# Last group's matrix-memory output turned by DVE and transfers, and turned blocks read a step later

## The chip, the cores and the metric

One core of a Trainium2 chip runs the kernel. The metric is device time in microseconds (us) of one execution; a profiled execution also leaves a trace of every engine: TensorE (PE, with its weight loads PEld), VectorE (DVE), ScalarE (ACT), GpSimd (POOL) and the queue of SyncE (SP), which issues most transfers.

## The reference, cut to what matters

One decoder layer, 256 tokens by 1024 channels, float32. An input projection feeds two branches: a matrix memory (mLSTM, 4 heads of 256) and an attention (MoBA, 8 heads of 128). Each branch has its own output projection; the two are gated, summed, projected, and followed by a layer norm and a gated MLP.

```python
proj = jnp.einsum("bsd,dn->bsn", x, w_in) + b_in
q_m, k_m, v_m, o_m, i_m, f_m, q_b, k_b, v_b, g_a, g_b = _split_cols(proj, SPLIT_SIZES)
...
h_m = mlstm_chunkwise(...)
y_a = (jax.nn.sigmoid(o_m) * head_norm(h_m, mlstm_norm)).astype(x.dtype)
h_b = moba_attention(...)
merged = (jax.nn.sigmoid(g_a) * jnp.einsum("bsw,wd->bsd", y_a, w_branch_a)
          + jax.nn.sigmoid(g_b) * jnp.einsum("bsw,wd->bsd", y_b, w_branch_b))
return jnp.einsum("bsd,de->bse", merged, w_out)
```

`head_norm` normalises each head's 256 channels of a token. With 256 tokens the attention is one causal block, so it is a plain causal softmax with a bias.

## The kernel before

The weights are a stream of 81 chunks of 128 x 2048 float32 (1 MB each), numbered s, one chunk a step, in a written order. Steps 0 to 3 are the output gate. Then come four groups g = 0 to 3 of eight steps each, from step 4 + 8g: `qm, qb, km, kb, vm, vb, ga, gb`. A group covers one memory head and two attention heads. Steps 36 to 43 are the branch projections (`wa, wa, wb, wb` twice: `wa` for the memory branch, `wb` for the attention), 44 to 47 the output projection, then the MLP.

Every float32 matmul is made of three in a rounded format: a value is split into a high part and the rest, and `mm3` issues high x high, rest x high, high x rest. So each weight chunk goes through `split`: ACT casts `raw` to `wh`, DVE subtracts to `wl`. The buffers `raw`, `wh` and `wl` have three places each. At step s the chunk s + 2 is split and the load of chunk s + 5 is issued on SP's queue; that load takes the place of `raw` of chunk s + 2, so it waits for that split.

All instructions are emitted in program order, by hand. At step s, `elem_work(s)` first emits what ACT, DVE and POOL do: the evacuation of step s - 1 (`evac`), side work put there by the groups (`side_elem`), interleaved with the split parts by the functions in `mixed` (a `None` in such a list stands for the next split part). Then come the load, the matmuls of step s (`step_*`), and the groups' own matmuls (`side_pe`). Each engine, and SP's queue, works in that order; semaphores make it wait.

A group's own work, by the names in `group_schedule`:
- `pe_s`, `el_w`, `el_s`: scores of the memory. `pe_n` makes the numerators `psn0`, `psn1` (tokens on partitions) in PSUM. `el_n1` takes mean, variance and denominator from them, `el_n1b` writes the centred and gated rows `yt` and the scale `scl`, `el_n2` scales `yt` on ACT. The rows must then be turned (channels on partitions) into `yah` and `yal` by `el_y`; the first `wa` step multiplies them, two 128-columns of each group.
- `pe_l(i)`, `el_l(i)`, `el_e(i)`, `el_l2(i)`: logits and softmax `lg` of attention head i. The block is turned, `el_t(i)` splits it into `pth`, `ptl`, `ptf`, `pe_o` multiplies them with the values into `pso`, `el_o` writes `ybh`, `ybl` for the `wb` steps.

A block is turned by `turn(i)` (i = 0, 1 the attention heads, 2 the memory): DVE transposes 32 x 32 tiles into `turn`, SP writes that to `flip` in DRAM, and four reads bring it back in its place. The reads are queued on SP right behind the write and wait until it has landed. In group 3 the memory's rows are not turned in this way: `pe_y` transposes them by four PE matmuls into `psy`, between steps 35 and 36.

`pe_o` stands behind the matmuls of the tenth step from the group's start, in group 3 behind those of the ninth, step 36.

Of the kernel before, what the change touches and what calls it, by code (L numbers as in the profile page):

```python
# [18 lines left out]
P = 128  # L19
S = 256  # L20
D = 1024
KT = D // P
# [50 lines left out]
class Kernel:  # L73
# [69 lines left out]
    def mm3(self, ps, ah, al, bh, bl, start, stop, first=None, only=(0, 1, 2)):  # L143

        a = (ah if first is None else first, ah, al)
        b = (bh, bl, bh)
        for i in only:
            self.nc.tensor.matmul(ps, a[i], b[i], start=start and i == 0, stop=stop and i == 2)  # L148

# [30 lines left out]
    def run(self):  # L180
# [132 lines left out]
        for s, (kind, i) in enumerate(self.order):  # L313
            if kind == "qm":
# [7 lines left out]
                      for i, (m, n) in enumerate(((1, 3), (1, 3), (2, 2))[:3 if g < NG - 1 else 2])] for g in range(NG)]  # L322
# [15 lines left out]
        for s, (kind, i) in list(enumerate(self.order))[4:]:  # L338
# [25 lines left out]
            parts = [] if late else self.split_parts(s + 2)  # L364
            if s == first["wa"] - 1:
                self.kept, parts = parts[-1], parts[:-1]
# [269 lines left out]
    def turn(self, t, d):  # L636
# [7 lines left out]
        self.nc.sync.dma_start(d.rearrange("m p f -> p m f"), tmp.rearrange("p (m f) -> p m f", m=m))  # L644
        t = t.rearrange("p c s -> p (c s)").rearrange("p (k f) -> p k f", k=4 * m)
# [4 lines left out]
    def group_schedule(self, g):  # L650
# [93 lines left out]

        def turn(i):
            self.turn(st["p", i] if i < 2 else st["yt"].rearrange("p t (j d) -> p (t j) d", j=2), self.flip[g][i])

        def pe_y():
            psy = self.ps_side([P, 2, S], f"psy{g}")
            for j in range(2):  # L750
                for t in range(2):
                    nc.tensor.transpose(psy[:, j, t * P:(t + 1) * P], st["yt"][:, t, j * P:(j + 1) * P], self.ident)
            st["psy"] = psy

        def el_y():
            for j in range(2):
                c = 2 * g + j
                gain = self.vec[:, V_NORM + c:V_NORM + c + 1]
                h, l = self.yah[:, c, :], self.yal[:, c, :]
                if last:  # L760
                    y = st["psy"][:, j, :]
                else:
                    y = st["yt"].rearrange("p t s -> p (t s)").rearrange("p (m k) -> p m k", k=64)[:, :, 32 * j:32 * j + 32]
                    h, l = (t.rearrange("p (m i) -> p m i", i=32) for t in (h, l))
                a.activation(h, y, AF.Copy, scale=gain)
                v.scalar_tensor_tensor(l, y, gain, h.bitcast(F32), op0=ALU.mult, op1=ALU.subtract)
# [90 lines left out]
        if g == 0:  # L857
            at(self.side_elem, 6, lambda: self.floor_exp())
        at(self.side_elem, 5 + o, lambda: turn(0))
        self.mixed[b + 6 + o] = lambda w: ([lambda: el_l(1), lambda: el_e(1), el_n1] + w  # L860
                                           + [lambda: el_l2(1), el_n1b, lambda: turn(1)])
        if last:
            self.mixed[b + 7] = lambda w: [el_n2, lambda: el_t(0)] + w
            at(self.side_pe, 7, pe_y)
            self.mixed[b + 8] = lambda w: [el_y, self.kept, lambda: el_t(1)] + w
        else:
# [24 lines left out]
    def step_wa(self, s, c, *a):  # L891
        nc = self.nc
        ps = self.ps_main(f"ps_wa{c}")
        self.mm_feat(s, ps, self.yah, self.yal)

        def evac():
            ga = self.sg["ga"][:, 2 * c:2 * c + 2, :]
            nc.scalar.activation(ga, ga, AF.Sigmoid)
            nc.vector.tensor_mul(ga, ps, ga)
# [421 lines left out]
```

## Time and profile before

| | |
|---|---|
| median of 3 runs | 478.13 us (477.64 to 479.82) |
| profiled execution | 478.69 us, its span 476.7 us |
| PE busy | 469.3 us, 98% of the span |
| DVE busy | 368.1 us, 77% |
| ACT busy | 309.7 us, 65% |
| POOL busy | 37.4 us, 8% |
| transfers | 97.35 MB, 204 GB/s in the mean |

The span is from the first to the last instruction; the execution's time has some 2 us around it. Rows of an engine's timeline read: start in us, length in us, engine, line of the kernel, operation, output<-input, shape, number of instructions merged, and in brackets the idle time before it with what ended it. For SP's queue the length is that of issuing; landing comes later. Rows of the chain that ended last: start, length, engine, output, line, count. Rows of stretches (A:B): length, busy time of PE, PEld, DVE, ACT and POOL, granted PE clock, share of the DMA engines, GB/s. L148 is the one line that issues nearly all matmuls, L94 and L95 the cast and the subtraction of every split, L89 the weight loads, L644 and L648 the write and the reads of a turn.

### The profile page before, as it was taken

The numbers are of one execution on the slowest core, as the hardware profiler recorded it, in microseconds if no ns is written. First come the engines' busy times: TensorE is split into PE (matmuls) and PEld (weight loads), VectorE is DVE, ScalarE is ACT, GpSimd is POOL, SyncE is SP. The second block draws the span as 40 slices with busy tenths as digits, with TensorE's granted clock in tenths as the row PEclk, the third lists the DMA queues.
The fourth block names the chain that finished last, engine by engine and source line by source line (L and its number), as shares of the span: only waits on it lengthen the run. The fifth ranks groups of instructions, "written<-read, shape, count | busy, mean of one in ns | idle before, by whom it ended". The sixth has DMA issues, their size and how long they took to land.

```text
span 476.7 us, 9493 instructions
## 1 busy us (share of the span) xinstructions
PE 469.3 (98%) x3788; PEld 454.8 (95%) x3788; DVE 368.1 (77%) x644; ACT 309.7 (65%) x540; POOL 37.4 (8%) x74
## 2 busy tenths in 40 slices
PE   8999999999999999999999999999999999999994
PEld 6999999999999999999999999999999999999984
DVE  4786979597869786986685898879668666778876
ACT  5669878597859786977663623765555545556871
POOL 0316501000200020010100001000000000000000
PEclk9999999999999999999999999999999999999999
DMA  7985665775666567655967472736564545456202
GB/s 232 324 298 180 212 239 162 222 276 195 173 239 247 193 171 253 234 169 177 368 243 260 148 294 88 268 101 252 184 236 170 206 178 192 171 214 219 89 0 89
DMA packets 28958, 97.35 MB, mean 204 GB/s; under 512 B 10581, under 2 KB 15585, under 8 KB 19697
## 3 DMA queue, kind: packets, MB, share of 16 engines
q1 hardware_dynamic: 27682, 92.51, 55.3%
q0 software_dynamic: 1232, 4.24, 2.7%
q8 instruction: 29, 0.48, 0.4%
q14 instruction: 15, 0.12, 0.1%
HBM read 93.31 MB, written 3.42 MB: 203 GB/s over the span
## 4 chain that ended last, share of the span: by engine, by line
PE 98%; DVE 0%; ACT 0%; DVEq 0%; issue 0%; ACTq 0%
PE ps_up L148 25%; PE ffn L148 13%; PE ps_ga L148 5%; PE ps_kb L148 5%; PE ps_vm L148 5%; PE mix L148 5%; PE ps_km L148 5%; PE ps_gb L148 5%; PE ps_wa L148 5%; PE ps_vb L148 5%; PE ps_wb L148 5%; PE ps_qm L148 5%; PE ps_qb L148 5%; PE ps_o0a L427 1%; PE ps_o0b L427 1%; PE psn L148 1%
## 5 line engine op out<-in xcount | busy, mean ns | idle before, releaser
L95 DVE TENSOR_TENSOR wl<-raw,wh 128x1024 fp32r<-128x1024 f32 (+4 forms) x147 | 180.0, 1261 | 26.8 <-ACT wh L94 24.5
L94 ACT CAST wh<-raw 128x1024 fp32r<-128x1024 f32 (+4 forms) x147 | 151.8, 1077 | 9.3 <-DMA raw<-in_wst_dram 4.0
L148 PE MATMUL ps_up<-x1h,wl 128*128 128x256 f32 x320 | 88.5, 276 | 0.0
L148 PE MATMUL ps_up<-x1h,wh 128*128 128x256 f32 x320 | 88.4, 276 | 0.0
L148 PE MATMUL ps_up<-x1l,wh 128*128 128x256 f32 x320 | 88.4, 276 | 0.0
L148 PEld LDWEIGHTS ps_up<-x1l,wh 128*128 128x128 f32 x320 | 60.1, 188 | 0.4
L148 PEld LDWEIGHTS ps_up<-x1h,wh 128*128 128x128 f32 x320 | 60.1, 188 | 0.3
L148 PEld LDWEIGHTS ps_up<-x1h,wl 128*128 128x128 f32 x320 | 60.1, 188 | 0.0
L1092 DVE SCALAR_TENSOR_TENSOR cu<-ps_up,vec,cu 128x255 f32<-128x255 f32 (+1 forms) x80 | 33.1, 476 | 20.1 <-ACT cu L1088 20.1
L148 PE MATMUL ffn<-wh,hl 128*128 128x512 f32 (+2 forms) x94 | 35.5, 378 | 0.0
L148 PE MATMUL ffn<-wl,hh 128*128 128x512 f32 (+2 forms) x94 | 35.5, 377 | 0.0
L148 PE MATMUL ffn<-wh,hh 128*128 128x512 f32 (+2 forms) x94 | 35.3, 375 | 0.0
L94 ACT CAST hh<-cu 128x256 fp32r<-128x256 f32 x22 | 8.9, 406 | 40.4 <-DVE cu L1103 40.4
L1088 ACT ACTIVATE cu<-ps_up,vec 128x256 f32<-128x256 f32 x40 | 16.7, 470 | 22.0 <-PE ps_up L148 22.0
L148 PEld LDWEIGHTS ffn<-wh,hl 128*128 128x128 f32 x94 | 17.7, 188 | 3.2
L148 PEld LDWEIGHTS ffn<-wl,hh 128*128 128x128 f32 x94 | 17.7, 188 | 3.1
L148 PEld LDWEIGHTS ffn<-wh,hh 128*128 128x128 f32 x94 | 17.7, 188 | 3.0
L990 POOL TENSOR_TENSOR rs<-rs,mhalf 128x1 f32<-128x1 f32 x3 | 2.1, 700 | 230.2 <-DVE rs L989 230.2
L148 PE MATMUL ps_ga<-xth,wh 128*128 128x256 f32 x64 | 18.0, 281 | 0.0
L148 PE MATMUL mix<-wh,mgh 128*128 128x256 f32 x64 | 17.8, 279 | 0.0
L148 PE MATMUL ps_wa<-yah,wh 128*128 128x256 f32 x64 | 17.8, 277 | 0.0
L148 PE MATMUL ps_kb<-xth,wl 128*128 128x256 f32 x64 | 17.7, 277 | 0.0
(344 smaller groups left out, 1476.6 us busy)
## 6 DMA issues: line engine op xcount, KB each, us to landing
raw<-in_wst_dram SPq DMA_DIRECT2D x72, 1024.0 KB, 4.9
raw<-in_wst_dram SPq DMA_DIRECT2D x10, 512.0 KB, 6.7
raw<-in_wst_dram SPq DMA_DIRECT2D x8, 256.0 KB, 4.5
lnrow<-in_rows_dram POOLq DMA_DIRECT2D x4, 512.0 KB, 6.9
flip<-turn SPq DMA_DIRECT2D x8, 192.0 KB, 3.2
lg<-flip SPq DMA_DIRECT2D x32, 48.0 KB, 2.0
xraw<-in_xt_dram SPq DMA_DIRECT2D x8, 128.0 KB, 4.0
toe<-table POOLq DMA_DIRECT2D x4, 256.0 KB, 4.7
```

What stands on the lines that cost most here:

```text
L94: self.nc.scalar.copy(wh, raw)
L95: self.nc.vector.tensor_sub(wl, raw, wh.bitcast(F32))
L148: self.nc.tensor.matmul(ps, a[i], b[i], start=start and i == 0, stop=stop and i == 2)
L427: mm(ps[t], x[:, k, t * P:(t + 1) * P], w, start=start and k == 0, stop=stop and k == KT - 1)
L990: nc.gpsimd.tensor_tensor(st["rs"], st["rs"], self.mhalf[:, 0:1], op=ALU.pow)
L1088: act.activation(cu[:, j, :], ps[:, j, :], AF.Copy, scale=tap(2, j))
L1092: v.scalar_tensor_tensor(cu[:, j, o:], ps[:, j, :S - o], tap(t, j), cu[:, j, o:], op0=ALU.mult, op1=ALU.add)
```

## The change

- The turn is cut in two: `turn` (transposes and write) and `turn_in` (the four reads). `back(i)` issues the reads a step after `turn(i)`.
- In groups 0 to 2, `el_t`, `el_y`, `pe_o` and `el_o` are moved later: to step 12 or 13 of the group's count in groups 0 and 1 (the `vm` and `vb` steps of the next group), to 10 and 12 in group 2.
- In group 3 the memory's rows are turned as in the other groups (`flip[3][2]`), and `pe_y` is gone. In step 34 `el_n1` and `el_n1b` stand first on DVE, then the split of chunk 35 (kept back from step 33), then `el_n2`, `turn(2)`, its reads `back(2)`, and then the second attention head's softmax, with the split of chunk 36 within it. `turn(1)` ends that step; its reads are issued in step 35.
- The first `wa` step uses `mm_late`: both halves over columns 0 to 5 first, then both over 6 and 7, which are the last group's. Its halves lie in two PSUM banks, and are evacuated by two multiplies.

```diff
+    def mm_late(self, s, ps, xh, xl, n):
+        wh, wl = self.w.pop(s)
+        for ks in (range(n), range(n, KT)):
+            for j in range(2):
+                for k in ks:
+                    a = self.col(s, k * 256 + j * P)
+                    self.mm3(ps[j], wh[:, a:a + P], wl[:, a:a + P], xh[:, k, :], xl[:, k, :], k == 0, k == KT - 1)
...
+            if s == first["wa"] - 3:
+                self.kept, parts = parts, []
             if s == first["wa"] - 1:
                 self.kept, parts = parts[-1], parts[:-1]
...
         self.nc.sync.dma_start(d.rearrange("m p f -> p m f"), tmp.rearrange("p (m f) -> p m f", m=m))
+
+    def turn_in(self, t, d):
+        m, _, f = d.shape
         t = t.rearrange("p c s -> p (c s)").rearrange("p (k f) -> p k f", k=4 * m)
...
         def turn(i):
-            self.turn(st["p", i] if i < 2 else st["yt"].rearrange("p t (j d) -> p (t j) d", j=2), self.flip[g][i])
-
-        def pe_y():
-            psy = self.ps_side([P, 2, S], f"psy{g}")
-            for j in range(2):
-                for t in range(2):
-                    nc.tensor.transpose(psy[:, j, t * P:(t + 1) * P], st["yt"][:, t, j * P:(j + 1) * P], self.ident)
-            st["psy"] = psy
+            return lambda: self.turn(*blocks(i))
+
+        def back(i):
+            return lambda: self.turn_in(*blocks(i))
...
-        at(self.side_elem, 5 + o, lambda: turn(0))
-        self.mixed[b + 6 + o] = lambda w: ([lambda: el_l(1), lambda: el_e(1), el_n1] + w
-                                           + [lambda: el_l2(1), el_n1b, lambda: turn(1)])
+        at(self.side_elem, 5 + o, turn(0))
         if last:
-            self.mixed[b + 7] = lambda w: [el_n2, lambda: el_t(0)] + w
-            at(self.side_pe, 7, pe_y)
+            self.mixed[b + 6] = lambda w: ([back(0), el_n1, el_n1b, *self.kept, el_n2, turn(2), back(2), lambda: el_l(1),
+                                            None, None, lambda: el_e(1)] + w + [lambda: el_l2(1), turn(1)])
+            self.mixed[b + 7] = lambda w: [lambda: el_t(0), back(1)] + w
             self.mixed[b + 8] = lambda w: [el_y, self.kept, lambda: el_t(1)] + w
-        else:
-            self.mixed[b + 8] = lambda w: [el_n2, lambda: el_t(0), lambda: turn(2)] + w
-            self.mixed[b + 9] = lambda w: w[0:1] + [lambda: el_t(1)] + w[1:]
-            at(self.side_elem, 10, el_y)
-        at(self.side_pe, 8 + o, pe_o)
-        at(self.side_elem, 9 + o, el_o)
+            at(self.side_pe, 8, pe_o)
+            at(self.side_elem, 9, el_o)
+            return
+        self.mixed[b + 7] = lambda w: ([back(0), lambda: el_l(1), lambda: el_e(1), el_n1] + w
+                                       + [lambda: el_l2(1), el_n1b, turn(1)])
+        self.mixed[b + 8] = lambda w: [back(1), el_n2, turn(2)] + w
+        self.mixed[b + 9] = lambda w: [back(2)] + w
+        k = 10 if g == NG - 2 else 12
+        for i in range(2):
+            at(self.side_elem, k, lambda i=i: el_t(i))
+        at(self.side_pe, k, pe_o)
+        at(self.side_elem, k, el_y)
+        if k == 10:
+            self.mixed[b + k] = lambda w: w[:-1] + [None, None] + w[-1:]
+        at(self.side_elem, 13 if k == 12 else 12, el_o)
...
-        self.mm_feat(s, ps, self.yah, self.yal)
+        if c == 0:
+            half = [ps[:, 0, :], self.ps_side([P, 2, 256], f"ps_wa{c}b")[:, 0, :]]
+            self.mm_late(s, half, self.yah, self.yal, KT - 2)
+        else:
+            self.mm_feat(s, ps, self.yah, self.yal)
```

How the order moves at the two places that the prediction speaks of. SP's queue from step 33 to step 35 (`flip30`, `flip31`, `flip32` are the writes of the last group's `turn(0)`, `turn(1)`, `turn(2)`; `lg6`, `lg7`, `yt3` the reads; `raw38` the load of chunk 38), before:

```order
L644 DMA flip30_426<-turn_2788 128x384
L648 DMA lg6_2770<-flip30_426 32x4x96 x4
L89 DMA raw38_2799<-in_wst_dram 128x2048
L644 DMA flip31_427<-turn_2903 128x384
L648 DMA lg7_2868<-flip31_427 32x4x96 x4
L89 DMA raw39_2914<-in_wst_dram 128x2048
L89 DMA raw40_2976<-in_wst_dram 128x2048
```

and now:

```order
L655 DMA flip30_426<-turn_2789 128x384
L89 DMA raw38_2792<-in_wst_dram 128x2048
L663 DMA lg6_2771<-flip30_426 32x4x96 x4
L655 DMA flip32_428<-turn_2892 128x2x256
L663 DMA yt3_2868<-flip32_428 32x8x64 x4
L655 DMA flip31_427<-turn_2918 128x384
L89 DMA raw39_2921<-in_wst_dram 128x2048
L663 DMA lg7_2900<-flip31_427 32x4x96 x4
L89 DMA raw40_2985<-in_wst_dram 128x2048
```

The reads `lg6` have moved behind the load of chunk 38; `flip32` and its reads are new and stand ahead of `flip31`; the reads `lg7` have moved behind the load of chunk 39.

DVE from the transpose of the first attention head's block, in step 33, on (`wl35` is the rest of chunk 35's weights, `lg7` and `mx7` belong to the second head's logits, `psn` are the numerators), before:

```order
L642 STREAM_TRANSPOSE turn_2788<-lg6_2770 128x3x4x32
L95 TENSOR_TENSOR wl35_2764<-raw35_2560,wh35_2763 128x1024 x2
L793 ISA lg7_2868,mx7_2869<-psl3_1_2850,toe_406 128x128
L793 ISA mx7_2869 128x1
L793 ISA lg7_2868,mx7_2869<-psl3_1_2850,toe_406 128x256
L793 ISA mx7_2869 128x1
L795 TENSOR_SCALAR mx7_2869<-mx7_2869 128x2
L715 BN_STATS bs3_2880<-psn0_3_2855 128x6
```

and now, in step 34, from the first row that writes `yt3` on (ahead of it stand that transpose and the statistics `bs3`, `den3`, `mv3`):

```order
L745 SCALAR_TENSOR_TENSOR yt3_2868<-psn0_3_2848,mv3_2865,sigo_105 128x256
L748 TENSOR_TENSOR scl3_2867<-mv3_2865,den3_2866 128x2
L745 SCALAR_TENSOR_TENSOR yt3_2868<-psn1_3_2849,mv3_2865,sigo_105 128x256
L749 TENSOR_TENSOR scl3_2867<-scl3_2867,den3_2866 128x2
L750 TENSOR_SCALAR scl3_2867<-scl3_2867 128x2
L95 TENSOR_TENSOR wl35_2765<-raw35_2548,wh35_2764 128x1024 x2
L653 STREAM_TRANSPOSE turn_2892<-yt3_2868 128x2x4x32 x2
L804 ISA lg7_2900,mx7_2901<-psl3_1_2843,toe_406 128x128
```

`wl35` has moved from ahead of the second head's logits (`lg7`) to behind the statistics and `scl`; the second head's logits stand behind the new transposes of `yt3`.

More of the change, by code (lines that the diff above doesn't have):

```diff
@@ L321, in run @@
         self.flip = [[dram.tile([m, P, n * P], F32, name=f"flip{g}{i}")
-                      for i, (m, n) in enumerate(((1, 3), (1, 3), (2, 2))[:3 if g < NG - 1 else 2])] for g in range(NG)]
+                      for i, (m, n) in enumerate(((1, 3), (1, 3), (2, 2)))] for g in range(NG)]
         self.gates_schedule(bif)
@@ L743, in el_n2, with blocks @@
                 a.activation(yt[:, t, :], yt[:, t, :], AF.Copy, scale=scl[:, t:t + 1])
+        def blocks(i):
+            return st["p", i] if i < 2 else st["yt"].rearrange("p t (j d) -> p (t j) d", j=2), self.flip[g][i]
         def turn(i):
-            self.turn(st["p", i] if i < 2 else st["yt"].rearrange("p t (j d) -> p (t j) d", j=2), self.flip[g][i])
-        def pe_y():
-            psy = self.ps_side([P, 2, S], f"psy{g}")
-            for j in range(2):
-                for t in range(2):
-                    nc.tensor.transpose(psy[:, j, t * P:(t + 1) * P], st["yt"][:, t, j * P:(j + 1) * P], self.ident)
-            st["psy"] = psy
+            return lambda: self.turn(*blocks(i))
+        def back(i):
+            return lambda: self.turn_in(*blocks(i))
         def el_y():
@@ L759, in el_y @@
                 h, l = self.yah[:, c, :], self.yal[:, c, :]
-                if last:
-                    y = st["psy"][:, j, :]
-                else:
-                    y = st["yt"].rearrange("p t s -> p (t s)").rearrange("p (m k) -> p m k", k=64)[:, :, 32 * j:32 * j + 32]
-                    h, l = (t.rearrange("p (m i) -> p m i", i=32) for t in (h, l))
+                y = st["yt"].rearrange("p t s -> p (t s)").rearrange("p (m k) -> p m k", k=64)[:, :, 32 * j:32 * j + 32]
+                h, l = (t.rearrange("p (m i) -> p m i", i=32) for t in (h, l))
                 a.activation(h, y, AF.Copy, scale=gain)
@@ L858, in group_schedule @@
             at(self.side_elem, 6, lambda: self.floor_exp())
-        at(self.side_elem, 5 + o, lambda: turn(0))
-        self.mixed[b + 6 + o] = lambda w: ([lambda: el_l(1), lambda: el_e(1), el_n1] + w
-                                           + [lambda: el_l2(1), el_n1b, lambda: turn(1)])
+        at(self.side_elem, 5 + o, turn(0))
         if last:
-            self.mixed[b + 7] = lambda w: [el_n2, lambda: el_t(0)] + w
-            at(self.side_pe, 7, pe_y)
+            self.mixed[b + 6] = lambda w: ([back(0), el_n1, el_n1b, *self.kept, el_n2, turn(2), back(2), lambda: el_l(1),
+                                            None, None, lambda: el_e(1)] + w + [lambda: el_l2(1), turn(1)])
+            self.mixed[b + 7] = lambda w: [lambda: el_t(0), back(1)] + w
             self.mixed[b + 8] = lambda w: [el_y, self.kept, lambda: el_t(1)] + w
-        else:
-            self.mixed[b + 8] = lambda w: [el_n2, lambda: el_t(0), lambda: turn(2)] + w
-            self.mixed[b + 9] = lambda w: w[0:1] + [lambda: el_t(1)] + w[1:]
-            at(self.side_elem, 10, el_y)
-        at(self.side_pe, 8 + o, pe_o)
-        at(self.side_elem, 9 + o, el_o)
+            at(self.side_pe, 8, pe_o)
[13 more added lines that the diff above has]
+        at(self.side_elem, 13 if k == 12 else 12, el_o)
     def open_post(self, pp):
@@ L898, in evac @@
             nc.scalar.activation(ga, ga, AF.Sigmoid)
-            nc.vector.tensor_mul(ga, ps, ga)
+            if c == 0:
+                for j in range(2):
+                    nc.vector.tensor_mul(ga[:, j, :], half[j], ga[:, j, :])
+            else:
+                nc.vector.tensor_mul(ga, ps, ga)
         self.evac[s] = evac
```

## The prediction

> **What bounds the kernel now.** I read the profile's first page, the list of waits of TensorE (PE), the chain that ended last, and then the rows of each engine around the last group.
>
> ```profile
> span 476.7 us, 9493 instructions
> PE 469.3 (98%) x3788; PEld 454.8 (95%) x3788; DVE 368.1 (77%) x644; ACT 309.7 (65%) x540; POOL 37.4 (8%) x74
> PE 98%; DVE 0%; ACT 0%; DVEq 0%; issue 0%; ACTq 0%
> PE warm_ps L202 <- DVE warm L199: 1.3, 1, 1.3
> ```
>
> The last row is the whole list of PE's waits: one wait, before the first matmul. PE is busy 98% of the span and is 98% of the chain, so the time is the sum of its matmuls. Two consequences: nothing that is made shorter on another engine can shorten the kernel, and any new wait of PE lengthens it one for one. The chain at the last group:
>
> ```profile
> 208.21 1.08 PE psn L148 x9
> ...
> 214.74 5.44 PE ps_gb L148 x48
> 220.18 0.44 PE psy L752 x4
> 220.62 5.47 PE ps_wa L148 x48
> ...
> 265.34 19.04 PE mix L148 x168
> ```
>
> Steps 33 (`vb`), 34 (`ga`), 35 (`gb`), 36 and 37 (`wa`) follow without a gap. I measure PE by starts of matmuls in its row-by-row timeline:
>
> ```profile
> 220.02 0.60 PE L752 MATMUL psy<-ident,yt 128*128 128x128 f32 x4
> 226.76 0.37 PE L826 MATMUL pso<-ptl,vbh 128*128 128x256 f32 x1
> ...
> 227.09 0.28 PE L148 MATMUL ps_wa<-yah,wh 128*128 128x256 f32 x1
> ```
>
> The second `wa` step starts at 227.09. That start is the mark: what moves it moves the end, for all after it is unchanged PE work.
>
> **The change, part by part.**
>
> *Four PE transposes go.* 0.44 us (chain row above). This is the only PE work removed, so the largest possible gain is 0.44 us, 0.1%.
>
> *The first `wa` step in another order, into two banks.* Still 48 matmuls. No row shows this very order; the `mix` row holds a run that alternates banks, at 19.04/168 = 113 ns against 5.47/48 = 114 ns. I take zero, bounds -0.05 and +0.05 us. Its evacuation becomes two multiplies on DVE, beside step 37.
>
> *Groups 0 to 2: reads, `el_t`, `pe_o` and `el_y` later.* PE does the same matmuls at another place. ACT and DVE lose a wait:
>
> ```profile
> 139.61 0.91 ACT L765 ACTIVATE yah<-yt,vec 128x256 fp32r<-128x256 f32 x2 [3.73 <-DMA yt<-flip]
> 163.11 0.56 DVE L694 TENSOR_TENSOR spl<-wt,sph 128x384 fp32r<-128x384 f32 x1 [0.23 <-ACT sph L688]
> 165.47 1.07 PE psn L148 x9
> ```
>
> ACT stood 3.73 us here for the turned block. The moved work (two `pth`, two `ptf`, two `yah`, some 2 us) goes into the next group's `vm` step, behind a chain that now runs earlier by about that wait. On SP's queue the reads move behind one load each; the latest, the `yt` reads of group 2, are used after two casts of that step, no earlier than now. The first thing PE would wait for there is `spl`: done at 163.67, used from 165.47, a margin of 1.8 us. I cost this at nothing; without that cover a microsecond of delay beyond 1.8 would cost a microsecond, in two groups.
>
> *The split of step 35's weights moves from step 33 to step 34, behind the statistics.* ACT's casts wait for nothing new. DVE's order in step 34 is now statistics, `yt`, scale, then two `wl`:
>
> ```profile
> 207.30 2.36 DVE L95 TENSOR_TENSOR wl<-raw,wh 128x1024 fp32r<-128x1024 f32 x2 [0.36 <-ACT wh L94]
> 210.32 0.76 DVE L715 BATCH_NORM_STATS2 bs<-psn 128x6 f32<-128x256 f32 x2
> 211.73 0.42 DVE L95 TENSOR_TENSOR vbl<-ps_vb,vbh 128x256 fp32r<-128x256 f32 x1
> ...
> 213.17 0.17 DVE L735 TENSOR_SCALAR scl<-scl 128x2 f32<-128x2 f32 x1
> ```
>
> The second `bn_stats` can start when `psn` ends, about 209.5. From its start (210.32 + 0.38 = 210.70) to the end of the scale (213.34) were 2.64 us, of which `vbl` (0.42) is no longer there: 2.2. So the scale ends at 211.7 and the two `wl` at 214.1. Step 35 starts at 214.74 and wants the second half 1.4 us later: hidden, by 0.6 us and 2 us.
>
> *What the last group adds, and what queues behind it.* Added are two transposes on DVE, a write and four reads on SP, all off PE, with rows below. On SP's queue the load of `raw38` needs the buffer that this split frees, so it is issued at 214.2, and behind it in the same queue now stand: four reads `lg6`, the write `flip32`, four reads `yt3`, the write `flip31`, load `raw39`, four reads `lg7`. These are the rows on how such transfers follow each other:
>
> ```profile
> 155.43 4.93 SPq L89 DMA_DIRECT2D raw<-in_wst_dram  x2
> ...
> 167.78 1.75 SPq L648 DMA_DIRECT2D lg<-flip  x4
> 169.63 0.38 SPq L89 DMA_DIRECT2D raw<-in_wst_dram  x1
> ...
> 175.36 1.75 SPq L648 DMA_DIRECT2D lg<-flip  x4
> 177.21 0.38 SPq L89 DMA_DIRECT2D raw<-in_wst_dram  x1
> 177.69 0.38 SPq L644 DMA_DIRECT2D flip<-turn  x1
> 183.33 1.80 SPq L648 DMA_DIRECT2D yt<-flip  x4
> ...
> 206.96 0.33 SPq L644 DMA_DIRECT2D flip<-turn  x1
> 208.87 2.62 SPq L648 DMA_DIRECT2D lg<-flip  x4
> ```
>
> Reads start when the write has landed. With the queue empty ahead of it a write takes 1.9 us (206.96 to 208.87). Right behind a load it takes 5.6 (177.69 to 183.33), and what stays the same is the distance from the load: 183.33 - 177.21 = 6.1, 175.36 - 169.63 = 5.7, and at worst 167.78 - 160.0 = 7.8 (the second load of the pair). A small transfer does not pass a load.
>
> The Trainium skill, "DMA: Bandwidth & Descriptors", section "Queues, rings and completion order", says why one would see this: descriptors of an engine are taken in ring order, and a transfer's semaphore increment lands only after every earlier write of that DMA engine. By that rule `flip32` could not be seen before `raw38` has landed, 214.2 + 5.3 = 219.5, and the sum would be at least +1.6 us; without it, a write of 1.9 us, it would be about -0.3. The rows agree with the rule.
>
> So `flip32`, issued near 216.4 (214.2 + 0.4 + 1.75 for the `lg6` reads; its transposes are done by 215.4), lands at t = 214.2 + 6.1 + 0.5 = 220.8. The 0.5 is an estimate for the 192 KB of `lg6` ahead of it at the highest rate that a stretch shows:
>
> ```profile
> 20.00:28.00 8.00, 8.00 (x52) 7.23 (x51) 5.29 (x8) 4.53 (x8) 0.77 (x2) 1.00 1.04 374
> raw<-in_wst_dram SPq DMA_DIRECT2D x1, 1024.0 KB, 5.3
> 186.90 0.91 ACT L765 ACTIVATE yah<-yt,vec 128x256 fp32r<-128x256 f32 x2 [2.84 <-DMA yt<-flip]
> 187.44 0.89 DVE L766 SCALAR_TENSOR_TENSOR yal<-yt,vec,yah 128x256 fp32r<-128x256 f32 x2 [2.74 <-ACT yah L765]
> 215.54 0.91 ACT L743 ACTIVATE yt<-yt,scl 128x256 f32<-128x256 f32 x2 [0.39 <-POOL scl L737]
> 174.18 0.77 DVE L642 STREAM_TRANSPOSE turn<-yt 128x256 f32<-128x256 f32 x2
> 216.36 0.39 ACT L94 CAST pth<-lg 128x256 fp32r<-128x256 f32 x1
> 216.78 0.43 DVE L95 TENSOR_TENSOR ptl<-lg,pth 128x256 fp32r<-128x256 f32 x1 [0.19 <-ACT pth L94]
> ```
>
> (The 215.4: POOL gave the scale 2.2 us after DVE's, 213.34 to 215.54, so 213.9, then 0.91 on ACT and the last transpose 0.4. Behind them DVE has the second head's logits, 0.7 from 209.66 to 210.32 before, `wl36`, 2.36, and `vbl`, 0.42: to 218.9, and ACT's copy of the same bank some 0.4 more. That bank is the first `wa` step's, from 220.02: hidden, by 0.7 us.)
>
> *First stall: `el_y`.* From the first `yt` read to `yah` were 3.57 us (183.33 to 186.90), to the end of the second `yal` 5.0 (188.33). So it is ready at t + 5.0 = 225.8. PE, without the transposes, starts step 36 at 220.02 and comes to columns 6 and 7, 36 matmuls later, at 224.1; it needs the second `yal` as its fifth matmul there, and 8 of 113 ns are left from that one: step 36 ends at 226.7 instead of 225.5. Stall 1.2 us.
>
> *Second stall: `el_t(1)`, then `pe_o`.* SP issues the `yt` reads until t + 1.8, `flip31` at once, `raw39` at t + 2.2; `raw39` needs 5.3 us and the `lg7` reads stand behind it: landed at t + 2.2 + 5.3 + 0.4 = t + 7.9. The other way round, without any queueing: `flip31` lands at t + 1.8 + 2.1, reads and use 3.6 to 3.8 later, t + 7.6. Both ends are close; I take 7.9. `pth` and `ptl` take 0.85 (216.36 to 217.21), and from the `ptl` matmul to the next step are 0.33 (226.76 to 227.09): step 37 starts at t + 9.2 with a hand-over of 0.1, that is 230.0. Without this stall `pe_o` would end at 226.7 + 1.2 = 227.9, so it costs 2.1 us.
>
> **Sum**: -0.44 + 1.2 + 2.1 = +2.9 us (230.0 against 227.09). The profiled execution took 478.69 us, its span and 2.0 us around it that stay; with the sum 481.6. The median of the runs shown is 478.13, 0.1% less; on it 481.0 us.
>
> Bounds: t with a distance of 5.7 and nothing for `lg6`, and 8.7 on to step 37: 228.6, +1.5. With 7.8 + 0.5, and one set of reads issued slowly (2.62 instead of 1.75) and a further 0.5 behind `raw39`: 222.5 + 10.6 = 233.1, +6. I stay near the lower end because two of three distances lie at 5.7 to 6.1.
>
> **The rivals.** A is the forecast.
>
> B, not slower: the small transfers pass the load. Place: `flip32`. If it lands within 2 us of its issue, at 218.3, step 37 starts at about 218.3 + 8.7 = 227.0, and the transposes' 0.44 is all but kept: 477.7 to 478.1. It decides at t = 218.4. For it: 1.9 us with an empty queue. Against it: every write behind a load above.
>
> C: step 35's weights come late. PE needs the first `wl` at 215.0, it ends at 212.9. A wait of DVE for POOL or ACT of more than 2 us ahead of it would cost what exceeds that, and A's chain starts there: one microsecond more gives 482. Against it: nothing stands between.
>
> D: PE's clock falls in the gaps.
>
> ```profile
> 5.08 0.41 PE L427 MATMUL ps_o2a<-wh,xtl 128*128 128x256 f32 x1
> 5.29 0.41 PE L427 MATMUL ps_o2b<-wh,xtl 128*128 128x256 f32 x1
> 470.00:476.70 6.70, 0.60 (x6) 0.39 (x4) 2.23 (x6) 0.86 (x3) 0.19 (x1) 0.86 0.22 78
> ```
>
> Matmuls at the start step by 0.21 us instead of 0.113, and the granted clock of the idle tail is 0.86. A clock lost for some 4 us of work would cost about 1.9 us more, 482.9. Against it: the longest gap in A is about 1.9 us, that of the tail 6. The Trainium skill, "TensorE: Matmul & The Clock Gate", "Part 1: The HAM clock gate", puts the gate at an idle window of about 3.4 us; by that rule it stays open here.
>
> E: groups 1 and 2 stall on `spl` despite the margin of 1.8 us: some 0.5 us each, 482.
>
> **How the numbers follow.** A 0.70, B 0.17, C 0.05, D 0.05, E 0.03. A's own range is 479.6 to 484.1, most of it 480.0 to 482.5. To hold 8 in 10 the range goes down to B, 477.7, and up to 483.2. A difference under 0.5%, 2.4 us, is about what a measurement of this kernel cannot tell from none. In A that line lies at t = 220.3, and I put 0.7 of A above it: 0.49, with most of C, D and E 0.60 slower. B and the rest of A make 0.38 for no change; 0.02 is left for faster, for no term gains more than 0.44.
>
> **What would show it.** PE's list of waits, with one entry before, would name `yah` or `yal` at L148 with about 1 us, and `pth` or `ptl` in `pe_o` with about 2. SP's queue would show a load issued near 214.2, the last `yt` reads near 220.8, the last `lg` reads near 225. Groups 0 to 2 show no wait of PE. The prediction is wrong if PE's list names no new wait, if the `yt` reads start before 218.4, or if a wait stands at step 35 or at `psn`.

## The result, and the profile after

The changed kernel takes 485.68 us (median of five executions, 484.67 to 485.84), the kernel before, run beside it, 478.76 us (477.64 to 479.82): ratio 1.0141, 95% interval 1.0125 to 1.0158. It is slower by 6.9 us; 2.9 were forecast. Two executions with a far lower mean clock, 0.17 (the profiled one of `e9_pool_queue`, whose trace is therefore not read) and 0.66 (one of the kernel before), are left out of all times.

The first page and the list of PE's waits of the changed kernel:

```profile
span 484.1 us, 9493 instructions
PE 471.8 (97%) x3784; PEld 456.8 (94%) x3784; DVE 369.0 (76%) x647; ACT 309.9 (64%) x540; POOL 37.5 (8%) x74
...
PE pso L835 <- ACT pth L94: 3.5, 1, 3.5
PE warm_ps L211 <- DVE warm L208: 1.3, 1, 1.3
PE ps_o0a L438 <- ACT wh L94: 0.8, 1, 0.8
PE ps_wa L148 <- ACT yah L776: 0.4, 1, 0.4
```

Four instructions fewer on PE, and two waits that the forecast named: `yah` in the first `wa` step, and `pth` in `pe_o` (the third row is at the start, where such a wait comes and goes between executions). But PE's busy time has *grown* by 2.5 us, 469.3 to 471.8, with less work. The chain of the changed kernel shows where:

```profile
207.83 1.09 PE psn L148 x9
...
230.54 0.58 PE pso L835
231.12 0.43 PE pso L836 x2
...
231.97 7.70 PE ps_wa L148 x48
```

and the same step in the chain of before:

```profile
227.25 5.44 PE ps_wa L148 x48
```

Step 37 starts 4.7 us later, and its 48 matmuls take 7.70 us instead of 5.44. A stretch of before (length, then busy time of PE, PEld, DVE, ACT, POOL, then the granted PE clock, DMA share, GB/s):

```profile
230.00:235.00 5.00, 5.00 (x46) 5.00 (x45) 4.53 (x6) 4.56 (x6) 0.00 (x0) 1.00 0.97 385
```

The same columns of the changed kernel say what stretched them:

```profile
225.00:230.00 5.00, 2.01 (x16) 1.80 (x16) 1.39 (x2) 0.59 (x1) 0.00 (x0) 0.98 0.90 306
230.00:232.00 2.00, 1.46 (x7) 1.46 (x8) 0.42 (x1) 1.92 (x5) 0.00 (x0) 0.50 0.50 197
232.00:234.00 2.00, 2.00 (x11) 2.00 (x11) 1.61 (x2) 1.98 (x3) 1.46 (x3) 0.50 0.05 20
234.00:236.00 2.00, 2.00 (x11) 2.00 (x11) 1.47 (x4) 1.60 (x3) 0.38 (x1) 0.50 0.86 279
236.00:238.00 2.00, 2.00 (x17) 2.00 (x16) 1.00 (x4) 1.54 (x3) 0.00 (x0) 0.84 1.03 387
```

PE's clock is granted by half from about 229.8 (0.98 over the first 5 us) to 236.6 (0.84 in the last row); it falls 0.7 us ahead of the end of the gap. Before, it reads 1.00 there. SP's queue before, with the load of chunk 38, the write `flip31` and the reads `lg7`:

```profile
211.58 0.38 SPq L89 DMA_DIRECT2D raw<-in_wst_dram  x1
213.90 0.34 SPq L644 DMA_DIRECT2D flip<-turn  x1
217.42 1.74 SPq L648 DMA_DIRECT2D lg<-flip  x4
```

and now:

```profile
213.45 0.33 SPq L89 DMA_DIRECT2D raw<-in_wst_dram  x1
213.87 1.85 SPq L663 DMA_DIRECT2D lg<-flip  x4
215.82 0.38 SPq L655 DMA_DIRECT2D flip<-turn  x1
220.23 1.79 SPq L663 DMA_DIRECT2D yt<-flip  x4
222.11 0.40 SPq L655 DMA_DIRECT2D flip<-turn  x1
222.62 0.38 SPq L89 DMA_DIRECT2D raw<-in_wst_dram  x1
224.13 1.74 SPq L663 DMA_DIRECT2D lg<-flip  x4
```

These are the load of chunk 38, the reads `lg6`, the write `flip32`, the reads `yt3`, the write `flip31`, the load of chunk 39 and the reads `lg7`, which are issued 6.7 us later than before. ACT then waits for the two landings (idle time and what ended it in brackets):

```profile
223.74 0.91 ACT L776 ACTIVATE yah<-yt,vec 128x256 fp32r<-128x256 f32 x2 [1.67 <-DMA yt<-flip]
...
230.08 0.40 ACT L94 CAST pth<-lg 128x256 fp32r<-128x256 f32 x1 [4.49 <-DMA lg<-flip]
```

### The profile page after: what moved, and what is told of

Same layout as the page of the kernel before. It is cut to its first block, busy times and chain, and to the rows that moved or that the text cites. A ratio compares the mean times of both kernels' runs of the same rounds, so it can differ in the third digit from the quotient of the medians.

```text
span 484.1 us, 9493 instructions
## 1 busy us (share of the span) xinstructions
PE 471.8 (97%) x3784; PEld 456.8 (94%) x3784; DVE 369.0 (76%) x647; ACT 309.9 (64%) x540; POOL 37.5 (8%) x74
## 4 chain that ended last, share of the span: by engine, by line
PE 93%; DMA 3%; SPq 1%; DVE 1%; ACT 1%; issue 0%; DVEq 0%; ACTq 0%
PE ps_up L148 25%; PE ffn L148 13%; PE ps_kb L148 5%; PE mix L148 5%; PE ps_vm L148 5%; PE ps_vb L148 5%; PE ps_wb L148 4%; PE ps_qm L148 4%; PE ps_km L148 4%; PE ps_qb L148 4%; PE ps_wa L148 4%; PE ps_ga L148 3%; PE ps_gb L148 3%; DMA lg<-flip 2%; PE ps_o0a L438 1%; PE ps_o0b L438 1%
## 5 line engine op out<-in xcount | busy, mean ns | idle before, releaser
L148 PE MATMUL ps_ga<-xth,wl 128*128 128x256 f32 x64 | 17.7, 277 | 0.0
```

## The experiments

The theory: the late split of chunk 35 makes SP's queue late, the gap at `pe_o` follows from the queue, and the gap takes the clock with it, which is a price beside the wait. Rivals: the changes of groups 0 to 2 cost too; the clock falls for another reason; the queue is not what makes `lg7` late.

### Which part of the change: e3_split35_early, e4_groups_only

`e3_split35_early` keeps the whole change but the late split; `e4_groups_only` keeps only groups 0 to 2 (group 3, its four transposes and the first `wa` step as before).

```diff
 # e3_split35_early
             if s == first["wa"] - 3:
-                self.kept, parts = parts, []
+                self.kept = []
```

> The split of chunk 35 goes back to step 33, nothing else. Theory T: the load of chunk 38 is issued near 208.5 and has landed when flip32 is written; yt reads start near 217, no wait at wa; flip31 is then bound by DVE's transpose (220), lg7 reads near 222, behind the load of chunk 39 (220.4), landing 6 to 7.4 after it, 226.4 to 227.8: gap 1 to 2.6 us, no clock loss, 479.3 to 480.8 us, ratio 1.002 to 1.005. Rival R1 (the late split is the whole cause): no gap at all, ratio 0.999.

> Groups 0 to 2 as in the changed kernel (reads and uses later), group 3 and the first wa step as before. Theory T and R1: no wait of PE, 478.0 to 478.8 us, ratio 1.000. Rival R4 (part of the loss is in groups 0 to 2): 480 us or more, ratio 1.004, with a wait of PE at psn or pso before 200 us.

Measured: 478.91 us, ratio 1.0015 (0.9999 to 1.0030), and 478.50 us, 0.9994 (0.9981 to 1.0007). Groups 0 to 2 cost nothing that can be told, as forecast. The gap that the theory still expected with the early split did not come, its rival held: taking back the late split alone takes back nearly all of the loss. SP's queue with the early split, and the chain at step 37:

```profile
208.65 0.33 SPq L89 DMA_DIRECT2D raw<-in_wst_dram  x1
...
216.09 1.79 SPq L663 DMA_DIRECT2D yt<-flip  x4
...
219.39 0.38 SPq L89 DMA_DIRECT2D raw<-in_wst_dram  x1
220.88 1.75 SPq L663 DMA_DIRECT2D lg<-flip  x4
```

```profile
227.04 5.46 PE ps_wa L148 x48
```

The load of chunk 38 goes out 4.8 us earlier, the reads `yt3` 4.1 and `lg7` 3.3 us. Nothing new on PE's list of waits, and step 37 is where it was. There is no slack in it, though: `lg7` is cast just as PE comes to it (end of the cast 226.02, first product 226.07), and the products then take 0.97 us instead of the 0.59 that they take in a row, so the 0.44 us of the transposes is lost again.

### What in the queue: e8_turn2_by_pe

The late split stays, but the memory's rows are turned by the four PE transposes, so `flip32` and the reads `yt3` are not in the queue.

```diff
-            el_n2, turn(2), back(2), lambda: el_l(1),
+            el_n2, lambda: el_l(1),
...
+            at(self.side_pe, 7, pe_y)
```

> Question: what do the two transfers of the memory outputs (flip32 and the four reads of yt) do in SP's queue, with the split as late as in the changed kernel? Here group 3's memory outputs are turned by four TensorE transposes as in the kernel before; all else is the changed kernel, late split and late load included. Theory T (lg7 is late because its blocks queue behind flip32, yt's reads and the 1 MB load): without the 0.4 us wait on yt's reads SP writes flip31 at about 220 instead of 222.1, lg7's reads are issued at about 222 and land 5 to 7 us later; the gap at pe_o is 0 to 1 us, the clock stays full; 478.7 to 479.7, ratio 1.000 to 1.003. Rival R1 (lg7's reads are held by the load ahead of them alone): flip31 is earlier but lg7 lands as late, gap 2 to 3.5 us, 483 to 486, ratio 1.009 to 1.016.

Measured: 480.87 us, ratio 1.0038 (1.0023 to 1.0053): between the two. Its wait and its step 37:

```profile
PE pso L845 <- ACT pth L94: 2.0, 1, 2.0
...
229.62 5.45 PE ps_wa L148 x48
```

The reads `lg7` are issued at 221.76, 2.4 us earlier than in the changed kernel, but land at 228.1: 6.3 us after their first issue and 2.0 after the load ahead of them (issued 220.26, landed 5.8 later). So the gap is larger than expected, 2.0 us. The clock stays full, in all seven executions (mean granted clock 0.996 to 0.999; in the five of the changed kernel 0.991 to 0.993). The time is that of the gap and of its restart and no more, 2.4 us by the medians and 1.8 by the ratio. With the late split in place, the transfers of the memory's rows thus bring the other 4.5 to 5 us; with the early split (`e3`) they cost next to nothing.

### Queue order or shared engines: e1, e9, e11, e12, e13

```diff
 # e1_load39_behind, and part of e12: the load of chunk 39 behind the reads lg7
-            self.load(s + 5)
+            if s != first["wa"] - 2:
+                if s == first["wa"] - 1:
+                    self.load(s + 4)
+                self.load(s + 5)
 # e11_swap, e12, e13: flip31 ahead of the reads yt3
-  turn(2), back(2), lambda: el_l(1), ... + w + [lambda: el_l2(1), turn(1)]
+  turn(2), lambda: el_l(1), ... + w + [lambda: el_l2(1), turn(1), back(2)]
 # e13_swap_act_queue: the reads lg7 issued by ACT; e9_pool_queue: flip31 and lg7 by POOL
-            self.nc.sync.dma_start(t[32 * b:32 * b + 32], src...)
+            (q or self.nc.sync).dma_start(t[32 * b:32 * b + 32], src...)
```

> Theory T (the load of chunk 39, issued 1.5 us ahead of the reads lg7 in the same queue, holds them back; the gap that PE then has before pe_o's second head costs 3.5 us and halves PE's clock for some 6 us more): the reads are used 3.6 us after their first issue, near 227.7, PE's gap is 1.2 us instead of 3.5, the clock stays at 1.00, wa's second step starts 5 us earlier than in the changed kernel: 480.5 us, ratio to before 1.004. Rival R1 (it is the lateness of the write flip31 that counts, and all of the queue is late because chunk 35 is split late): the reads still land near 230, ratio 1.014. Rival R2 (the transfers share one bandwidth, order in the queue does not matter): gap about 3 us, ratio 1.012.

> Question: is lg7 late because its transfers stand in one queue behind yt's reads and the 1 MB load, or because the DMA engines are shared with that load? The changed kernel, but flip31's write and lg7's four reads are issued from POOL's queue instead of SP's; the order on the other engines is as it was. Theory T (queue order): flip31 is written when DVE has turned it (about 219.5 to 220), the reads are issued about 2 us later and land 3 us after that, about 225 to 226: gap at pe_o 0 to 0.8 us, clock full, 478.7 to 480, ratio 1.000 to 1.003. Rival R1 (shared engines): the reads land 5 to 7 us after their issue as before, 228 to 229, gap 2 to 3 us and the clock falls: 483 to 485.5, ratio 1.009 to 1.015.

> Question: is it the place in SP's queue, or the landing of the 1 MB load ahead of them, that sets when lg7's reads land? The changed kernel with one swap in the queue: flip31's write ahead of the four yt reads instead of behind them; the load for step 39 still stands ahead of lg7's reads. In the runs so far lg7 landed 1 to 2.3 us after that load had landed (changed kernel: load issued 222.6, landed 5.4 later at 228.0, lg7 at 229.9; turned by TensorE: 220.3, 226.1, 228.1). Theory T (lg7 lands about 2 us behind the load, whenever its reads are issued): flip31 is written at about 220 instead of 222.1, lg7's reads are issued at 222.5 to 223 instead of 224.1, the load is still issued at 222 to 222.7, and lg7 still lands at 229.3 to 230; gap 3 to 3.6 us, the clock falls; 484.5 to 486, ratio 1.012 to 1.015. Rival R1 (the reads take 4 to 6 us from their own issue): lg7 lands at 227 to 228.5, gap 0.5 to 2, clock full, 479.5 to 481, ratio 1.002 to 1.005.

> Question: can the late split be kept if the queue is put right? The swap of the run before (flip31's write ahead of the yt reads), and the load for step 39 issued behind lg7's reads instead of ahead of them. Theory T (what costs is the order in SP's queue): lg7's reads are issued at about 222.3 with no load between them and flip31, and land about 3 us after the last is issued, at about 227; the gap at pe_o is 0 to 1 us, the clock stays full, the 0.4 us at wa stays; 478.8 to 480, ratio 1.001 to 1.004. Rival R1 (the two loads that now start right behind the reads slow them as much as the one ahead did): lands at 229 or later, gap 2 to 3.5, clock falls, 483 to 486. Rival R2 (load 39 is now late for its own step): a new wait of 1 us or more for wh or wl at a later step, ratio 1.003 or more with the gap gone.

> Question: do lg7's reads wait for the load because they stand in one queue with it, or because the DMA engines are busy with it? As the swap alone, but lg7's four reads are issued by ACT, just ahead of yah and yal's work, while the load for step 39 stays on SP; ACT is free at about 222, so the reads are issued at about 222.1 to 223.9, at the same time as the load. Theory T (queue order): they land 2 to 3 us after the last issue, at 226 to 227, before the load does; gap 0 to 0.6, clock full, 478.8 to 480, ratio 1.001 to 1.004 (yah may be 0.3 later, so up to 0.7 us at wa). Rival R1 (shared engines): they land with or behind the load, at 228 to 230; gap 1.5 to 3.5, 481 to 486, ratio 1.005 to 1.015.

| | us | ratio | gap at `pe_o`, us |
|---|---|---|---|
| e1_load39_behind | 484.43 | 1.0125 (1.0109 to 1.0142) | 2.1, clock falls |
| e9_pool_queue | 484.26 | 1.0124 (1.0098 to 1.0150) | not seen |
| e11_swap | 483.07 | 1.0102 (1.0077 to 1.0128) | 2.3, clock full in the trace |
| e12_swap_behind | 481.12 | 1.0048 (1.0031 to 1.0065) | none |
| e13_swap_act_queue | 483.28 | 1.0096 (1.0079 to 1.0113) | 2.0, clock full |

The load of chunk 39, the reads `lg7`, and ACT's first use of them: with the load ahead in the same queue (e11_swap),

```profile
222.69 0.39 SPq L89 DMA_DIRECT2D raw<-in_wst_dram  x1
223.19 1.80 SPq L663 DMA_DIRECT2D lg<-flip  x4
...
229.35 0.40 ACT L94 CAST pth<-lg 128x256 fp32r<-128x256 f32 x1 [3.28 <-DMA lg<-flip]
```

with the load at the same time in another queue (e13_swap_act_queue),

```profile
221.91 1.80 ACTq L663 DMA_DIRECT2D lg<-flip  x4
222.51 11.42 SPq L89 DMA_DIRECT2D raw<-in_wst_dram  x3
...
228.90 0.41 ACT L94 CAST pth<-lg 128x256 fp32r<-128x256 f32 x1 [2.96 <-DMA lg<-flip]
```

and with the loads behind in the same queue (e12_swap_behind):

```profile
222.39 1.81 SPq L666 DMA_DIRECT2D lg<-flip  x4
224.25 6.60 SPq L89 DMA_DIRECT2D raw<-in_wst_dram  x3
...
225.82 0.41 ACT L94 CAST pth<-lg 128x256 fp32r<-128x256 f32 x1
```

From the last read's issue to the use are 4.4 us, 5.2 us and 1.6 us; in `e1`, also with the loads behind, 2.8 us. A queue of its own does not help while the load runs (the theory's expectation for `e13` missed, its rival held; `e9`'s time says the same, less surely). What helps is to be issued ahead of the load: in `e13` the first of the four reads, issued 0.6 us ahead of it, landed after 1.9 us, the last two, issued behind it, after 5.9 and 5.6 us, and the load itself took 6.0. So the place in one ring is not needed to hold the reads: a load that is under way in another queue holds them as well. By what it does so is not shown. The load's data on the same DMA engines would do it, but in `e8`, where all stand in one queue, the engines are nearly idle (mean share 0.05) from 226.0 to 227.0, between the landing of the load and the reads' data, so busy engines are not the whole of it. `e11` missed too: 0.9 us of earlier issue gave 0.7 us of earlier landing, and since PE itself came to the wait 0.5 us later, the gap shrank from 3.5 to 2.3 us. In its four executions the mean clock was 0.998, 0.996, 0.994 and 0.991, with 482.35, 482.43, 483.71 and 485.34 us: near this length the same kernel loses the clock at one time and not at another.

`e1` missed: the queue still waits for `flip32` and then, alone, for `flip31` (reads `lg7` at 225.69), and the last of the reads, with the loads right behind it, takes 3.1 us to landing, the first two 1.8 and 1.9 (with the loads as close behind, the last one in `e5_both` takes 1.9); the gap of 2.1 us still took the clock, for one stretch of 3.4 us (mean granted clock 0.993 to 0.994 in all four executions). `e12` has no gap, but its time missed too, by 1.1 us: its step 37 starts 0.7 us behind that of before, and what else its profiled execution lost is told in the last section.

### The price of the clock: e2_fill20, e6_fill34, e7_pe_o_later

Matmuls whose result nothing reads are put into the gap of the changed kernel, 20 and 34 of 0.113 us.

```diff
                 mm(ps[:, i, :], vl[:, c], th, start=False, stop=True)
+                if last and i == 0:
+                    for _ in range(34):
+                        mm(self.spare, self.ybh[:, 0, 0:P], self.yah[:, 0, :], start=True, stop=True)
```

> This kernel adds 20 matmuls of 256 columns, into a part of PSUM that nothing reads, between the two heads of pe_o, where PE stands idle for 3.5 us. They need 2.3 us. Theory T (the clock is a price of the gap, by itself 2.9 us): the wait for pth ends at the same time, the idle gap is 1.3 us, the clock stays at 1.00, matmuls behind it step by 0.113 us: 482.8 us, ratio 1.008. Rival R3 (the clock falls for another reason, the gap is all that counts): no change, 485.7, ratio 1.014.

> Question: is the lost clock a price of its own, beside the wait? The changed kernel with 34 extra matmuls (128x256, result unread, 0.113 us each at full clock = 3.8 us) placed between the last ready output product and the wait on lg7, so that the gap of 3.5 us has work in it; the transfers and their order are untouched. Theory T (the loss is the wait, about 3.9 us with the 0.4 at wa, and beside it about 2.9 us of half clock that the gap sets off): the gap is under 0.6 us, the clock stays at 1.00, step wa of chunk 36 takes 5.4 to 5.5 us for 48 matmuls, the end of the wait is where it was; 482.5 to 483.0 us, ratio 1.008 to 1.009. Rival R1 (the half clock falls on its own, or for another reason than the gap): it falls although PE is busy, 485 to 486, ratio 1.013 to 1.016. Rival R2 (the clock costs nothing, all of the loss is later transfers): clock full and still 1.013 or more.

Measured: 485.00 us, ratio 1.0128 (1.0106 to 1.0151), and 484.58 us, 1.0128 (1.0100 to 1.0157). Both expected times missed, since `lg7` landed later than in the changed kernel (at 231.1 and 231.7 instead of 229.9): the load ahead of it took 7.5 and 6.9 us instead of 5.4. Why it did is open; the two kernels with extra matmuls are the only ones in which it took so long. By the times alone, two rivals would stand (no change in `e2`; full clock and still 1.013 in `e6`), but it is the longer wait that makes these times. What the runs were made for is seen in the trace all the same. Wait and step 37 of `e6_fill34`:

```profile
PE pso L835 <- ACT pth L94: 1.1, 1, 1.1
...
233.31 5.46 PE ps_wa L148 x48
```

Step 37 starts 1.3 us *later* than in the changed kernel, its 48 matmuls take 5.46 us instead of 7.70, and it ends 0.9 us earlier. In `e2_fill20` a gap of 2.3 us is left; the clock fell in one of its four executions.

`e7_pe_o_later` leaves the gap unfilled but moves `pe_o` behind step 37, and `el_o` a step later.

```diff
-            at(self.side_pe, 8, pe_o)
-            at(self.side_elem, 9, el_o)
+            at(self.side_pe, 9, pe_o)
+            at(self.side_elem, 10, el_o)
```

> Question: is the time lost only because PE reaches pe_o before lg7 has landed? The changed kernel with its late split, its loads and transfers as they are, but pe_o of group 3 is put behind the matmuls of step 37 instead of ahead of them, and el_o a step later; 5.4 us of matmuls then cover the wait. Theory T (the price is the gap at pe_o and the clock that it sets off; the transfers themselves cost nothing): the wait at pe_o is gone, the 0.4 us wait at wa stays, the clock stays at 1.00; 478.5 to 479.5, ratio 1.000 to 1.002. Rival R1 (the later end of the outputs is paid anyway, at wb, which reads ybh and ybl of group 3): a wait of 1 to 3 us appears at ps_wb, 480 to 483, ratio 1.004 to 1.010. Rival R2 (the clock falls whatever pe_o does, from the stall at yah): 481 or more.

Measured: 487.48 us, ratio 1.0182 (1.0160 to 1.0204). The theory missed and the first rival was too mild. PE's new waits:

```profile
PE ps_wb L148 <- ACT ybh L846: 2.3, 1, 2.3
PE ps_wb L148 <- DVE ybl L847: 1.2, 1, 1.2
```

The outputs are needed by the very next step, and `el_o` now stands behind ACT's two `wh` casts and the sigmoid; the two waits at `wb`, with one matmul between them, are together as long as that at `pe_o` was, and the clock falls there (0.59 at 240 to 242). A step of matmuls is no cover for a wait if the result is due right behind it.

### The gap alone: e5_both, e14_gap_1, e15_gap_3, e16_gap_5

`e5_both` is the early split with the load of chunk 39 behind `lg7`. On it, 9, 14 and 22 extra casts of `pth` hold PE up by ACT alone; the transfers up to the gap stay.

```diff
+            if last and i == 1:
+                for _ in range(9):
+                    a.copy(th, ps[:, 0:2])
             self.split_into(th, tl, ps[:, 0:2])
```

> Question: is there a version of the change that beats the kernel before? Chunk 35 split in step 33 again (as in the run of that name), and the load for step 39 put behind lg7's reads. Theory T (with the early split nothing on PE waits, so all that is left is 0.44 us of four transposes gone and what lies under the spread): lg7 lands at about 224 to 225, 1 us earlier than with the early split alone; no PE wait but that of the start, clock full; 478.2 to 478.9, ratio 0.999 to 1.001. Rival R1 (load 39 3 us later makes the weights of step 39 late): a wait for wh or wl of 0.5 to 2 us at wb, ratio 1.001 to 1.005.

> Question: what does a gap of PE at this place cost by itself? The version without any wait (early split, load 39 behind lg7's reads, 478.2 us), in which ACT casts lg7 to pth nine times more ahead of the cast that counts, 0.3 us each; the transfers are untouched. lg7 was there 1.4 us early, so the gap at pe_o is about 1.3 us. Theory T (a gap costs its length and 0.3 to 0.5 us for the restart, and beyond some 2 to 3.4 us also the clock): clock full, step 37 takes 5.4 to 5.5 us; 479.6 to 480.4, ratio 1.002 to 1.004. Rival R1 (the clock falls in any gap over 1 us): step 37 takes 6 us or more, 481.5 to 483, ratio 1.006 to 1.010.

> As the run with nine extra casts, with fourteen: a gap at pe_o of about 2.8 us, longer than the 1.9 that the prediction called safe and shorter than 3.4 us. Theory T (a stretch of about 3.4 us that PE works less than half of is enough for the clock to fall, for one or two such stretches at 1.7 us each): half clock in the rows right behind the gap, step 37 takes 6.5 to 7.8 us, 482.5 to 485, ratio 1.009 to 1.014, executions differing by up to 1.7 us. Rival R1 (the clock falls only behind a gap of 3.4 us or more, so what took it in the changed kernel was something else): step 37 5.4 to 5.5 us, clock full, 481.0 to 481.8, ratio 1.005 to 1.007.

> As the run with nine extra casts, with twenty-two: a gap at pe_o of about 5.2 us, longer than 3.4 us. Theory T: half clock for two such stretches behind the gap, 2.5 to 3.5 us beyond the gap; step 37 7 to 9 us; 486 to 488, ratio 1.016 to 1.020. Rival R1 (it falls only when a gap holds a whole window of 3.4 us, and 5.2 us does so in about half of the executions): executions in two groups 1.7 to 3 us apart, 483.5 to 487. Rival R2 (no clock loss by the gap alone): 483.3 to 484.2, ratio 1.010 to 1.012.

`e5_both` takes 478.24 us, ratio 0.9990 (0.9975 to 1.0005): no wait, and step 37 starts at 226.37, 0.88 earlier than before; 0.44 of it was there already at the start of step 33 (201.73 against 202.17), the other 0.44 is the four transposes, and it is too little to tell from no change. So the expectation held. No version here beats the kernel before.

In the trace the casts follow each other by 0.44 us, not 0.3, so the gaps came out longer than meant and the expected times missed:

| | gap, us | step 37, us | us | over `e5_both` | ratio |
|---|---|---|---|---|---|
| e14_gap_1 | 2.7 | 7.07 | 483.07 | 4.8 | 1.0108 (1.0065 to 1.0151) |
| e15_gap_3 | 4.8 | 6.41 | 484.78 | 6.5 | 1.0131 (1.0107 to 1.0155) |
| e16_gap_5 | 8.2 | 6.97 | 490.18 | 11.9 | 1.0254 (1.0221 to 1.0287) |

Gaps and step 37 are those of the profiled executions, times are medians. The profiled execution of `e16_gap_5` was its fastest, 488.19 us, 10.4 above that of `e5_both`: 8.2 of gap and 2.4 of slower matmuls behind it make 10.6. Stretches of `e14_gap_1`, where PE stood from 225.9 to 228.6:

```profile
226.00:228.00 2.00, 0.00 (x0) 0.00 (x0) 0.00 (x0) 1.87 (x5) 0.00 (x0) 1.00 0.98 406
228.00:230.00 2.00, 1.38 (x11) 1.37 (x11) 0.43 (x1) 1.97 (x6) 0.00 (x0) 1.00 0.71 299
230.00:232.00 2.00, 2.00 (x12) 2.00 (x11) 1.52 (x2) 1.98 (x3) 1.84 (x3) 0.52 0.42 41
232.00:234.00 2.00, 2.00 (x14) 2.00 (x12) 1.47 (x3) 1.68 (x3) 0.00 (x0) 0.63 0.80 330
234.00:236.00 2.00, 2.00 (x20) 2.00 (x19) 1.00 (x4) 1.46 (x3) 0.00 (x0) 1.00 1.04 352
```

By the gap alone, with no transfer ahead of it moved, the clock falls: a gap of 2.7 us is enough. It falls about 1.5 us after PE is back at work, and stays halved for some 3.4 us (1.9 us of it in the row of 230, from a mean of 0.52, and 1.5 in that of 232). The time fits a sum: the gap, 0.4 for the restart, and 1.6 of lost clock make 4.7 against 4.8 measured. The rival named for `e15`, a fall only behind gaps over 3.4 us, is refuted by `e14`, whose gap came out shorter than that.

## Why the prediction was wrong

The direction, the late queue and the two waits were right; the price of the second wait and of the clock was not. Measured against the start of `psn` in the profiled executions (207.83 against 208.21, so 0.38 is taken off):

| term | forecast | measured |
|---|---|---|
| four transposes | -0.44 | -0.44 (`e5_both`) |
| groups 0 to 2 | 0 | 0 (`e4_groups_only`) |
| split of chunk 35, PE's wait at step 35 | 0 | 0 |
| first stall, `yah` | +1.2 | +1.2: a wait of 0.4, and matmuls further apart around it |
| second stall, `pe_o` | +2.1 | +3.5, the wait |
| restart of `pe_o` | 0 | +0.4 |
| PE's clock | 0 | +2.7: step 37 7.70 for 5.44 or 5.46, and 0.46 in `pe_o` |
| start-up | 0 | -0.4, before the change has begun |
| sum | +2.9 | +7.0 |

*Right.* The first stall came as forecast. The load of chunk 38 was forecast at 214.2 and issued at 213.45, the first read of `yt3` at 220.8 and came at 220.23, `yah` 3.5 us later (forecast 3.57). So the chain from the late split through `flip32` to the two waits stands, and `e3_split35_early`, which takes that split back, takes back nearly the whole loss. B, small transfers that pass the load, is refuted: `flip32` landed 4.4 us after its issue. C and E did not come: neither step 35 nor `spl` is on the list of waits.

*Wrong, the larger part: the clock.* The step that failed is "any new wait of PE lengthens it one for one": the sum has no term for the clock, and 2.7 us of the loss are the clock's, beside the wait that set it off. D had 0.05 and its price was 1.9 us. By its own rows that price is too low: matmuls that step by 0.21 instead of 0.113 us lose 3.4 us on 4 us of work; 1.9 is what they lose in 4 us of time. Its chance was set by "the longest gap in A is about 1.9 us, that of the tail 6". Two errors are in that. The step put the margin on a length whose own bounds, +1.5 to +6 for the sum, were 4.5 us apart, and it took the only gap seen before (6 us in the tail) as the nearest case. The Trainium skill, "TensorE: Matmul & The Clock Gate", "Part 1: The HAM clock gate", speaks of an idle window of about 3.4 us, free-running; read as a gap of 3.4 us it says that 2.7 us are safe. The runs do not agree with that reading: 2.7 us set off the loss with the transfers ahead of it untouched (`e14_gap_1`), 2.0 us did not (`e8`, `e13`, eleven executions by their mean clock, 0.996 to 0.999), 2.1 us did in all four of `e1`, and at 2.3 us (`e2`, `e11`) it depends on the execution. Free-running windows fit what is seen: the fall lasts some 3.4 us, or two or three times that, and its start is not tied to the gap's end, 1.5 us behind PE's return in `e14_gap_1` and 0.7 ahead of it in the changed kernel. In `e14_gap_1` the 3.4 us ahead of the fall (226.7 to 230.1) hold 1.9 us of gap and 1.5 us of work: if the window that decides is the one that ends with the fall, being idle only in part was enough. No run shows which window decides.

*Wrong, the smaller part: a term of the second stall.* "t + 2.2 + 5.3 + 0.4" was the landing of `lg7`. The first two were 2.4 and 5.4, for the load has these values in the trace:

```profile
raw<-in_wst_dram SPq DMA_DIRECT2D x1, 1024.0 KB, 5.4
```

The 0.4 for four small reads behind the load was 1.9 (222.62 + 5.4 = 228.0; used at 230.08 after a landing at 229.9). In `e8` it was 2.0, in `e11` 1.1 (222.69 + 5.4 = 228.1; landed at 229.2). The reason given for the delay, order in one queue, is at most a part of it: the reads that ACT issued behind the load landed no earlier (`e13`). Of the rule that the prediction cited from the Trainium skill, "DMA: Bandwidth & Descriptors", "Queues, rings and completion order", the first half, ring order, is thus not needed for the delay; the second, that a transfer's semaphore increment lands only after every earlier write of that DMA engine, is stated there for all queues of the engine and agrees with `e13`. Whether it is that or the sharing of the engines stays open.

Without the clock the sum would have been +4.3 and the time 483, just under the range's upper end. That the gap, the largest uncertain term, could also set off the clock should have been a condition on that term, not a rival apart with its own small chance: over some 2 us of gap, the price jumps, by 1.6 us in `e14_gap_1` and 2.7 in the changed kernel.

## What to carry to other kernels

On a kernel that PE bounds, a wait of PE is not priced one for one: beyond about 2 us it took 1.6 to 2.7 us of clock as well in these runs, so keep new waits below that. Before a weight split or anything that frees a load's buffer is moved later, follow the load that it holds, and everything small that is due behind it; a small transfer needed soon must be issued ahead of a 1 MB load. Putting it into ACT's queue or, by its time, POOL's instead of SP's made no difference here. A result that is due in the next step cannot be hidden by moving both it and its reader by one step.

## What the runs showed of the hardware that was not expected

- The clock is taken back for about 3.4 us at a time, which costs up to 1.7 us of work. The changed kernel lost two such stretches behind 3.5 us of wait, `e15_gap_3` one behind 4.8 us, `e16_gap_5` three behind 8.2 us (228.1 to 238.4, from 2.5 us after PE stopped): the length of the gap alone does not set how many.
- The first products of `pe_o` behind a wait took 0.97 us with a full clock (`e8`: 228.65 to 229.62) and 0.59 without a wait.
- In some executions PE runs 4% slower for 35 to 60 us while its granted clock reads 1.00 and DVE and ACT keep their pace. The chain of `e12_swap_behind`, and of before:

```profile
244.90 11.31 PE ps_wa L148 x96
```

```profile
243.57 10.88 PE ps_wa L148 x96
```

It cost that execution some 2.2 us, from 0.7 behind at step 37 to 2.9 at the first MLP step, and accounts for most of that execution's loss; the other three of `e12` have no trace. The traces of `e2`, `e7` and `e13` have it from the same place on, that of `e1` from 70 to 104 us, ahead of all that was changed; the other traces, those of before and of the changed kernel among them, do not. The profiled executions of these five are slower by it. What sets it off is open.
